# Keys and values of four late heads by seven products of blocks, in a hybrid attention and convolution step

## The chip, the cores and the metric

The kernel runs on one core of one Trainium2 chip. The metric is the device time of one execution in microseconds; the median of the runs shown is compared. In three runs the kernel before took 1614.0 to 1616.18 us, with a median of 1615.59 us.

The engines are called TensorE (PE in the profile, its weight loads PEld), VectorE (DVE), ScalarE (ACT), GpSimd (POOL) and SyncE (SP). SyncE issues the weight loads, GpSimd most other transfers.

## The reference

One step of a decoder layer, for a prompt of 16 learned and 512 given rows and for 8 decoding sequences of 4 rows each, so 560 rows of 2048 columns:

```python
h = rmsnorm(x, g_pre)
q, k, v, ga, cb, cc, ch, gc, ma, mc = jnp.split(h @ w_in, split_offsets(), axis=-1)
a = attend(q, k, v, b_sb).reshape(bsz, t, D_ATTN) * jax.nn.silu(ga)   # 8 heads of 128, stick-breaking
u = cc * ch
c = cb * causal_conv(concat(conv_hist, u), w_conv, b_conv) * jax.nn.silu(gc)
merged = sigmoid(ma + b_gate[:D_MODEL]) * (a @ w_pa) + sigmoid(mc + b_gate[D_MODEL:]) * (c @ w_pc)
y = x + rmsnorm(merged @ w_out, g_post)
return y, k, v, u_ext[:, -(CONV_WIDTH - 1):]
```

`attend` gives key s to query t only for s < t, with the weight sigmoid(z_ts) * prod over s < j < t of (1 - sigmoid(z_tj)). The decoding rows attend to 512 cached keys and values each, in 4 pages of 128, besides their own. The keys and values of all 560 rows are outputs too. Everything is float32.

## The kernel before

**Numbers.** Every float32 operand of a large product is split in two halves that TensorE multiplies fast: `hi` (ScalarE, L240) and `lo = x - hi` (VectorE, L241). Three matmuls (hi hi, hi lo, lo hi) make one product. The split weights have three buffers each (`whl`), the raw weights five (`wraw`); a weight tile is 128 x 1024, eight blocks of 128 rows for 128 output columns.

**Stages.** First the norm fills `h_hi` and `h_lo` (h transposed, 16 blocks of 128 x 560), with the query projections of heads 0 to 3. Then `head_now` for heads 0 to 3: K projection (`k_proj`), V projection (`v_proj`), the query projection of the head that lies four further on, and the attention (`attend`). Then `head_later` for heads 4 to 7: K and V projections alone, K to the scratch `k_scr`, V to `vn_scr`. Such a plain projection (`proj`) computes 128 output columns for 560 rows in two halves of 280: 2 halves x 16 blocks x 3 = 96 matmuls, from two weight tiles.

**Seven products.** Behind the heads come the gates and the convolution's inputs, 72 blocks of 128 columns, in 36 pairs of 256 columns (`pair`, `seven`). A pair is a product of 2 x 2 blocks (rows of h in two halves, inputs in two halves, columns in two halves), and is computed with seven block products instead of eight, each of 8 x 3 = 24 matmuls, 168 a pair. For that three of the right sides are sums of blocks of h, in the tiles `t_hi[i]` and `t_lo[i]`, built once (L906 to L927, on chunks of two of eight blocks, VectorE's sums and ScalarE's `hi`); the fourth, `r1`, is written over block (0, 1) of `h_hi` and `h_lo` at the end. Four weight sums a pair (L953, L956, L964, L969) are made by VectorE, and seven weight tiles are split instead of four.

**The decode's pieces.** The decode attention is a generator (`decode_steps`), called by `dec_step` at many places: in 64 logit steps (each one page of cached keys for one sequence, four rows and four heads: 16 reduces on VectorE, L754), then the weights, then 16 groups of value products and their ends (L841, on TensorE, from `vpage` tiles). `DEC1 = 6` says that the logits of six of the 16 units (a unit has four steps) are made among the heads, and those of the other ten behind each group of gates, by the table in `dec_group`.

**Behind the gates** comes a stage over the 16 column blocks of `w_pc`, with the attention of heads 4 to 7 and the decode's value products between (`head_here`), and then `w_pa`, the merge and `w_out`.

**What sets the order.** The program is written in loops, and a scheduler orders the instructions of each engine when the kernel is built: it moves them past each other where data and buffers allow. On the chip each engine takes its instructions in that order, one behind the other, and waits where an input is not there. So a tile's `hi` and `lo`, the sums and the reduces stand in one queue on VectorE, and a matmul waits for the latest of its operands.

Of the kernel before, what the change touches and what calls it, by code (L numbers as in the profile page):

```python
# [17 lines left out]
P = 128  # L18
# [29 lines left out]
DEC1 = 6  # L48
# [12 lines left out]
def hybrid_step_kernel(  # L61
# [499 lines left out]
    def k_proj(h):  # L561
        o = proj(GATE_K + h * P, ALL)
        kr = hp.tile([P, T], F32, name="raw", bufs=2)
        for ob, s in nparts(o):
            act.copy(kr[:, s], ob)
# [11 lines left out]
    def v_proj(h, pl=None):  # L577
        o = proj(GATE_V + h * P, ALL)
        vr = hp.tile([P, T], F32, name="raw", bufs=2)
        for ob, s in nparts(o):  # L580
            act.copy(vr[:, s], ob)
# [109 lines left out]
    def head_now(h):  # L691
# [7 lines left out]
        q_proj(NOW + h)  # L699
        dec_step(2, "part")  # L700
# [5 lines left out]

    def head_later(h):
        pool.dma_start(k_scr[h], k_proj(h))
        dec_step(2, "part")
        v_proj(h)  # L710
        dec_step(2, "part")
# [20 lines left out]
    def decode_steps():  # L732
# [89 lines left out]
        for g in range(2):  # L822
            for hf in range(2):
                cs = slice(hf * 512, (hf + 1) * 512)
                po = t_ps()
                for pg in range(NPG + 1):
                    if pg < NPG:
                        vts = []
                        for j in range(4):
                            vt = d3.tile([P, 512], F32, name="vpage", bufs=7)  # L830
                            page_load(vt, vc, 4 * g + j, pg, cs)
                            vts.append(vt)
# [37 lines left out]
    def dec_group():  # L870

        n = n_group[0] = n_group[0] + 1
        if n <= 32:
            dec_step((0, 2, 2, 2)[n - 1] if n <= 4 else 1 if n <= 20 else 1 + n % 2, "logits")
# [9 lines left out]
    nctx.close()  # L884
    for h in range(NOW, H):
        head_later(h)
    dec_step(64, "part")
# [5 lines left out]
    for i in range(3):  # L893
        ttp = tctx.enter_context(tc.tile_pool(name=f"tt{i}", bufs=1))
        t_hi.append(ttp.tile([P, 8, HU], F32R, name=f"t_hi{i}"))
        t_lo.append(ttp.tile([P, 8, HU], F32R, name=f"t_lo{i}"))
    h_f, l_f = h_hi.bitcast(F32), h_lo.bitcast(F32)

    def blk(x, i, j):
        return x[:, 8 * i:8 * i + 8, (j + 1) * HC - HU:(j + 1) * HC]  # L900
# [5 lines left out]
    with tc.tile_pool(name="tsum", bufs=2, side="right") as tsp:  # L906
        r1 = tsp.tile([P, 8, HU], F32, name="r1", bufs=1)
        for c in range(0, 8, 2):
# [3 lines left out]
            r, x, y = part(r1), *(tsp.tile([P, 2, HU], F32, name=n) for n in "xy")  # L912
# [14 lines left out]
    hctx.close()  # L927


    def gate_out(j, w, g):  # L930
        pool.dma_start(gate_scr[j][:, w, :], g)

    def gate_bias(j, w):
        return bg[:, KD * w + j:KD * w + j + 1]
# [47 lines left out]
    def pair(c, n):  # L982
# [6 lines left out]
        def rt(i):  # L989
            return lambda k: (t_hi[i][:, k, HU - n:HU], t_lo[i][:, k, HU - n:HU])  # L990
# [3 lines left out]
        yield from seven(ws, n, rb, rt, s, lambda name: sp2.tile([P, HU], F32, name=name)[:, :n])  # L994
# [3 lines left out]
    sp2 = gctx.enter_context(tc.tile_pool(name="sums", bufs=1))  # L998
# [100 lines left out]
    gctx.close()  # L1099
    tctx.close()  # L1100
# [331 lines left out]
```

## Time and profile before

| | us |
|---|---|
| median of three runs | 1615.59 |
| the profiled execution | 1616.69 |
| its span on the chip | 1615.1 |
| TensorE busy | 1595.0 (99%) |
| VectorE busy | 1268.6 (79%) |
| ScalarE busy | 754.0 (47%) |
| mean granted clock of TensorE | 0.997 of full speed |

By time from the span's start: norm and first queries to about 78 us; attention of heads 0 to 3 to about 297; K and V of heads 4 to 7 to about 369; the 36 pairs to about 1112, at some 21 us each for most; the `w_pc` stage with heads 4 to 7 to about 1330; the rest to the end. The busy time of an engine counts overlapping instructions once. The spacing of two neighbouring instructions (start to start) is shorter than a row's duration, since one begins before the other's end is recorded.

### The profile page before, as it was taken

What the parts mean: (1) busy time and instruction counts of PE and PEld (TensorE: products, weight loads), DVE (VectorE), ACT (ScalarE), POOL (GpSimd) and SP (SyncE); (2) the same over time, 40 slices, a digit from 0 to 9 for tenths busy, and PEclk for the clock granted to TensorE, in tenths of its full rate; (3) what the DMA queues carried; (4) which work ended last, traced back from release to release, by engine and by line L of the source; (5) the groups of instructions that cost most, each with busy time, mean ns of one, the idle gap of its engine ahead of it and who ended that gap; (6) DMA issues with size and microseconds to landing.
All of it is one profiled execution on the core that took longest, in us unless ns stands there. A gap on an engine that the chain in (4) does not pass through costs nothing.

```text
span 1615.1 us, 32344 instructions
## 1 busy us (share of the span) xinstructions
PE 1595.0 (99%) x12172; PEld 1533.7 (95%) x12172; DVE 1268.6 (79%) x3574; ACT 754.0 (47%) x1339; POOL 238.0 (15%) x428
## 2 busy tenths in 40 slices
PE   9999999999999999999999999999999999999997
PEld 8999999999999999999999999999757789999997
DVE  6328999947899999999999986667565747887776
ACT  6335554435444444444454444446554523355562
POOL 1133333221111001001011100001322210000000
PEclk9999999999999999999999999999999999999999
DMA  8245555344554445454455544444966755533345
GB/s 244 85 139 179 162 173 177 114 121 142 163 166 138 137 139 164 119 151 133 139 171 183 155 145 128 130 127 124 334 218 222 232 152 162 173 88 110 99 133 187
DMA packets 300675, 252.77 MB, mean 157 GB/s; under 512 B 11522, under 2 KB 268614, under 8 KB 299702
## 3 DMA queue, kind: packets, MB, share of 16 engines
q1 hardware_dynamic: 272021, 160.45, 34.5%
q0 software_dynamic: 28368, 89.98, 16.8%
q8 instruction: 95, 1.56, 0.4%
q14 instruction: 63, 0.51, 0.1%
q10 hardware_dynamic: 128, 0.27, 0.1%
HBM read 217.95 MB, written 32.71 MB: 155 GB/s over the span
## 4 chain that ended last, share of the span: by engine, by line
PE 95%; DMA 2%; DVE 2%; ACT 1%; issue 0%; DVEq 0%; POOL 0%; SPq 0%; ACTq 0%
PE mm L941 31%; PE mm L256 27%; PE o L941 23%; PE tp L841 3%; PE mm L321 2%; PE z L677 1%; PE o L687 1%; PE z L321 1%; PE z L608 1%; PE z L1373 1%; DMA sg<-a_scr 1%; PE tp L505 0%; DMA raw<-in_w_pc 0%; DMA qb<-q_scr 0%; PE z L1227 0%
## 5 line engine op out<-in xcount | busy, mean ns | idle before, releaser
L240 ACT CAST whi<-raw 128x1024 fp32r<-128x1024 f32 x247 | 259.5, 1051 | 385.2 <-PE mm L941 118.5
L241 DVE TENSOR_TENSOR wlo<-raw,whi 128x1024 fp32r<-128x1024 f32 x247 | 301.8, 1223 | 87.8 <-ACT whi L240 86.5
L941 PE MATMUL mm<-h_hi,whi 128*128 128x272 f32 (+1 forms) x1152 | 332.3, 288 | 0.0
L941 PE MATMUL mm<-h_lo,whi 128*128 128x272 f32 (+1 forms) x1152 | 332.3, 288 | 0.0
L941 PE MATMUL mm<-h_hi,wlo 128*128 128x272 f32 (+1 forms) x1152 | 332.3, 290 | 0.0
L941 PE MATMUL o<-t_hi,whi 128*128 128x272 f32 (+1 forms) x864 | 250.1, 289 | 1.6 <-DVE c L967 1.6
L941 PE MATMUL o<-t_lo,whi 128*128 128x272 f32 (+1 forms) x864 | 250.2, 290 | 0.0
L754 DVE CUSTOM_DVE_ANT_0 junk<-kpage,qb 128x128 f32<-128x128 f32 x1024 | 246.3, 288 | 4.7 <-DMA qb<-q_scr 4.3
L941 PE MATMUL o<-t_hi,wlo 128*128 128x272 f32 (+1 forms) x864 | 249.8, 289 | 0.0
L941 PEld LDWEIGHTS mm<-h_hi,whi 128*128 128x128 f32 x1152 | 217.4, 189 | 0.0
L941 PEld LDWEIGHTS mm<-h_hi,wlo 128*128 128x128 f32 x1152 | 216.8, 189 | 0.1
L941 PEld LDWEIGHTS mm<-h_lo,whi 128*128 128x128 f32 x1152 | 216.8, 188 | 0.1
L241 DVE TENSOR_TENSOR wlo<-s,whi 128x1024 fp32r<-128x1024 f32 x126 | 154.4, 1225 | 63.6 <-ACT whi L240 62.4
L240 ACT CAST whi<-s 128x1024 fp32r<-128x1024 f32 x126 | 132.0, 1048 | 153.8 <-PE mm L941 51.7
L256 PE MATMUL mm<-h_lo,whi 128*128 128x280 f32 (+1 forms) x640 | 187.6, 293 | 0.0
L256 PE MATMUL mm<-h_hi,wlo 128*128 128x280 f32 (+1 forms) x640 | 187.1, 293 | 0.0
L256 PE MATMUL mm<-h_hi,whi 128*128 128x280 f32 (+1 forms) x640 | 186.7, 292 | 0.0
L941 PEld LDWEIGHTS o<-t_hi,whi 128*128 128x128 f32 x864 | 163.0, 189 | 2.1 <-DVE c L967 2.0
L941 PEld LDWEIGHTS o<-t_lo,whi 128*128 128x128 f32 x864 | 163.4, 189 | 0.4 <-issue 0.4
L941 PEld LDWEIGHTS o<-t_hi,wlo 128*128 128x128 f32 x864 | 163.1, 189 | 0.1
L256 PEld LDWEIGHTS mm<-h_lo,whi 128*128 128x128 f32 x640 | 120.3, 188 | 0.8
L256 PEld LDWEIGHTS mm<-h_hi,whi 128*128 128x128 f32 x640 | 120.5, 188 | 0.5
(390 smaller groups left out, 3214.5 us busy)
## 6 DMA issues: line engine op xcount, KB each, us to landing
raw<-in_w_in SPq DMA_DIRECT2D x192, 512.0 KB, 4.3
kpage<-in_cache_k POOLq DMA_DIRECT2D x64, 256.0 KB, 3.7
qb<-q_scr POOLq DMA_DIRECT2D x32, 512.0 KB, 5.7
vpage<-in_cache_v POOLq DMA_DIRECT2D x64, 256.0 KB, 5.4
raw<-in_w_out SPq DMA_DIRECT2D x32, 512.0 KB, 4.1
gate_scr<-g POOLq DMA_DIRECT2D x32, 272.0 KB, 4.8
gt<-gate_scr POOLq DMA_DIRECT2D x16, 544.0 KB, 4.5
raw<-in_w_pc SPq DMA_DIRECT2D x16, 512.0 KB, 7.3
```

The source lines that it names most:

```text
L240: act.copy(hi, x)
L241: dve.tensor_sub(lo, x, hi.bitcast(F32))
L256: pe.matmul(o, lhsT=w, rhs=r[:, t0:t1], start=(k == 0 and n == 0), stop=(k == nk - 1 and n == 2))
L321: pin(pe.matmul(o, lhsT=l, rhs=r[:, k, t0:t1], start=(start and m == 0), stop=(stop and m == 2), skip_group_check=True))
L608: pe.matmul(zt[:m, c0:c0 + n], lhsT=l[:, s0:s0 + m], rhs=r[:, ts:ts + n], start=(c0 == 0 and i == 0), stop=(i == 2), skip_group_check=True)
L677: pe.matmul(o, lhsT=l, rhs=x, start=False, stop=(i == len(ops) - 1), skip_group_check=True)
L687: pe.matmul(ot[:, ts - NMETA:ts - NMETA + n], lhsT=l[:m, st, :], rhs=x[:m, c0:c0 + n], start=False, stop=(g == GROUPS[-1] and i == 2), ski ...
L754: dve.tensor_tensor_reduce(out=junk, in0=kt[:, h * P:(h + 1) * P], in1=qt[:, t, h * P:(h + 1) * P], scale=1.0, scalar=0.0, op0=ALU.mult, o ...
L841: pe.matmul(po[32 * j:32 * (j + 1), :], lhsT=lhs, rhs=rhs, start=(pg == 0), stop=(pg == NPG), tile_position=(0, 32 * j), skip_group_check= ...
L941: pe.matmul(o, lhsT=l[:, k, :], rhs=r, start=(start and k == 0 and m == 0), stop=(stop and k == 7 and m == 2), skip_group_check=True)
L1373: pin(pe.matmul(o, lhsT=(m1, m2)[h][:, k + 8 * (q == 1), ts], rhs=two[h][q == 2][:, :, k, :], start=(n == 0), stop=(n == 47)))
```

## The change

- K and V of heads 4 to 7 are no longer computed by `proj` but in four pairs, two heads' K or two heads' V at a time (`two_heads`), by the same `seven` as the gates, on halves of 280 columns. `k_proj` and `v_proj` take their result as an argument.
- For that the t tiles are built on all 560 rows (`HC` = 280 columns for each half instead of `HU` = 274) and the build is written ahead of these pairs; the pool `sums` opens there too.
- The query projections of heads 4 to 7 are written behind the attention of heads 0 to 3, and no longer inside `head_now`.
- `DEC1` falls from 6 to 4: eight logit steps (two units) are no longer made among the heads but with the gates; `dec_group`'s table calls them.
- `vpage` has six buffers instead of seven.

```diff
@@ -45,7 +45,7 @@
 NPG = 4
 NPOOL = 40
 EPS = 1e-6
-DEC1 = 6
+DEC1 = 4
 SCRATCH = 4096
 FIRST = 4
 WARM = 10
@@ -558,11 +558,15 @@
         split_evac(vhi[0:16, 4, :], vlo[0:16, 4, :], vn[0:16, 4, :], vn[0:16, 4, :])
         return vhi, vlo
 
-    def k_proj(h):
-        o = proj(GATE_K + h * P, ALL)
-        kr = hp.tile([P, T], F32, name="raw", bufs=2)
-        for ob, s in nparts(o):
-            act.copy(kr[:, s], ob)
+    def whole(c):
+
+        r = hp.tile([P, T], F32, name="raw", bufs=2)
+        for ob, s in nparts(proj(c, ALL)):
+            act.copy(r[:, s], ob)
+        return r
+
+    def k_proj(h, kr=None):
+        kr = whole(GATE_K + h * P) if kr is None else kr
         kn = hp.tile([P, 5, P], F32, name="nat", bufs=2)
         ks = hp.tile([TS, P], F32, name="ks", bufs=1)
         natural(kr, kn, ks)
@@ -574,11 +578,8 @@
                        bias=bsb[0:TS, h:h + 1])
         return kr
 
-    def v_proj(h, pl=None):
-        o = proj(GATE_V + h * P, ALL)
-        vr = hp.tile([P, T], F32, name="raw", bufs=2)
-        for ob, s in nparts(o):
-            act.copy(vr[:, s], ob)
+    def v_proj(h, pl=None, vr=None):
+        vr = whole(GATE_V + h * P) if vr is None else vr
         vn = hp.tile([P, 5, P], F32, name="nat", bufs=2)
         vs = hp.tile([TS, P], F32, name="ks", bufs=1)
         natural(vr, vn, vs)
@@ -696,19 +697,12 @@
         dec_step(1 if h else 0, "part")
         vhi, vlo = v_proj(h, np_)
         dec_step(1, "part")
-        q_proj(NOW + h)
-        dec_step(2, "part")
+        dec_step(1, "part")
         ot = attend(np_, h, khi, klo, vhi, vlo, qr)
         dec_step(2, "part")
         at = np_.tile([P, PQ], F32, name="at", bufs=1)
         act.copy(at, ot)
         pool.dma_start(a_scr[h], at)
-
-    def head_later(h):
-        pool.dma_start(k_scr[h], k_proj(h))
-        dec_step(2, "part")
-        v_proj(h)
-        dec_step(2, "part")
 
     def head_loads(h):
         kr = hl[0].tile([P, T], F32, name="kr")
@@ -827,7 +821,7 @@
                     if pg < NPG:
                         vts = []
                         for j in range(4):
-                            vt = d3.tile([P, 512], F32, name="vpage", bufs=7)
+                            vt = d3.tile([P, 512], F32, name="vpage", bufs=6)
                             page_load(vt, vc, 4 * g + j, pg, cs)
                             vts.append(vt)
                         if g + hf + pg == 0:
@@ -871,7 +865,7 @@
 
         n = n_group[0] = n_group[0] + 1
         if n <= 32:
-            dec_step((0, 2, 2, 2)[n - 1] if n <= 4 else 1 if n <= 20 else 1 + n % 2, "logits")
+            dec_step((0, 2, 2, 2)[n - 1] if n <= 4 else 1 + n % 2, "logits")
         else:
             dec_step(1)
 
@@ -882,9 +876,9 @@
     for h in range(NOW):
         head_now(h)
     nctx.close()
+    dec_step(64, "part")
     for h in range(NOW, H):
-        head_later(h)
-    dec_step(64, "part")
+        q_proj(h)
 
 
 
@@ -892,24 +886,24 @@
     t_hi, t_lo = [], []
     for i in range(3):
         ttp = tctx.enter_context(tc.tile_pool(name=f"tt{i}", bufs=1))
-        t_hi.append(ttp.tile([P, 8, HU], F32R, name=f"t_hi{i}"))
-        t_lo.append(ttp.tile([P, 8, HU], F32R, name=f"t_lo{i}"))
+        t_hi.append(ttp.tile([P, 8, HC], F32R, name=f"t_hi{i}"))
+        t_lo.append(ttp.tile([P, 8, HC], F32R, name=f"t_lo{i}"))
     h_f, l_f = h_hi.bitcast(F32), h_lo.bitcast(F32)
 
     def blk(x, i, j):
-        return x[:, 8 * i:8 * i + 8, (j + 1) * HC - HU:(j + 1) * HC]
+        return x[:, 8 * i:8 * i + 8, j * HC:(j + 1) * HC]
 
     def t_split(hi, lo, x):
         act.copy(hi, x)
         dve.tensor_sub(lo, x, hi.bitcast(F32))
 
     with tc.tile_pool(name="tsum", bufs=2, side="right") as tsp:
-        r1 = tsp.tile([P, 8, HU], F32, name="r1", bufs=1)
+        r1 = tsp.tile([P, 8, HC], F32, name="r1", bufs=1)
         for c in range(0, 8, 2):
             def part(x, *ij):
                 return (blk(x, *ij) if ij else x)[:, c:c + 2]
 
-            r, x, y = part(r1), *(tsp.tile([P, 2, HU], F32, name=n) for n in "xy")
+            r, x, y = part(r1), *(tsp.tile([P, 2, HC], F32, name=n) for n in "xy")
             dve.tensor_sub(r, part(h_f, 0, 0), part(h_f, 0, 1))
             dve.tensor_add(r, r, part(l_f, 0, 0))
             dve.tensor_sub(r, r, part(l_f, 0, 1))
@@ -924,14 +918,7 @@
             t_split(part(t_hi[2]), part(t_lo[2]), x)
         for c in range(0, 8, 2):
             t_split(blk(h_hi, 0, 1)[:, c:c + 2], blk(h_lo, 0, 1)[:, c:c + 2], r1[:, c:c + 2])
-    hctx.close()
-
-
-    def gate_out(j, w, g):
-        pool.dma_start(gate_scr[j][:, w, :], g)
-
-    def gate_bias(j, w):
-        return bg[:, KD * w + j:KD * w + j + 1]
+
 
     def product(o, w, rhs, start, stop):
         hi, lo = w
@@ -987,15 +974,38 @@
             return lambda k: (h_hi[:, 8 * i + k, slice(*hs[j])], h_lo[:, 8 * i + k, slice(*hs[j])])
 
         def rt(i):
-            return lambda k: (t_hi[i][:, k, HU - n:HU], t_lo[i][:, k, HU - n:HU])
+            return lambda k: (t_hi[i][:, k, HC - n:HC], t_lo[i][:, k, HC - n:HC])
 
         ws = blocks_of(win, c)
         s = sp2.tile([P, 8, P], F32, name="s")
-        yield from seven(ws, n, rb, rt, s, lambda name: sp2.tile([P, HU], F32, name=name)[:, :n])
+        yield from seven(ws, n, rb, rt, s, lambda name: sp2.tile([P, HC], F32, name=name)[:, :n])
+
+    sctx = ExitStack()
+    sp2 = sctx.enter_context(tc.tile_pool(name="sums", bufs=1))
+
+    def two_heads(c):
+
+        rs = [hp.tile([P, T], F32, name="raw", bufs=2) for _ in range(2)]
+        for m, half, ob in pair(c, HC):
+            act.copy(rs[m][:, NMETA + half * HQ:NMETA + (half + 1) * HQ], ob[:, HM:HC])
+            act.copy(rs[m][:, half * HM:(half + 1) * HM], ob[:, 0:HM])
+        return rs
+
+    for h in range(NOW, H, 2):
+        for i, r in enumerate(two_heads(GATE_K + h * P)):
+            pool.dma_start(k_scr[h + i], k_proj(h + i, r))
+        for i, r in enumerate(two_heads(GATE_V + h * P)):
+            v_proj(h + i, vr=r)
+    hctx.close()
+
+    def gate_out(j, w, g):
+        pool.dma_start(gate_scr[j][:, w, :], g)
+
+    def gate_bias(j, w):
+        return bg[:, KD * w + j:KD * w + j + 1]
 
     gctx = ExitStack()
     gp = gctx.enter_context(tc.tile_pool(name="gates", bufs=2))
-    sp2 = gctx.enter_context(tc.tile_pool(name="sums", bufs=1))
 
 
     UP, US = PQ + 2, DB * (DT + 2)
@@ -1097,6 +1107,7 @@
     dec_step(64, "values")
     assert "values" in dec_at and "end" not in dec_at
     gctx.close()
+    sctx.close()
     tctx.close()
```

The whole program has 96 matmuls of TensorE less, 36 instructions of VectorE more (12 splits, 16 weight sums, 8 differences `c`) and 24 of ScalarE more; the number of transfers on SyncE's and GpSimd's queues is the same.

The order on VectorE, before, while K and V of heads 4 to 7 are projected. L913 to L923 are the t sums, L904 the `lo` of a t tile, L241 the `lo` of a weight tile:

```order
L915 TENSOR_TENSOR r_5282<-r_5282,h_lo 128x548 x3
L241 TENSOR_TENSOR wlo<-raw,whi 128x1024
L915 TENSOR_TENSOR r_5282<-r_5282,h_lo 128x548
L916 TENSOR_TENSOR x<-r_5282,h_hi 128x548 x2
L241 TENSOR_TENSOR wlo<-raw,whi 128x1024
L917 TENSOR_TENSOR x<-x,h_lo 128x548 x2
L919 TENSOR_TENSOR y<-h_hi,x 128x548 x2
L904 TENSOR_TENSOR t_lo_5268<-x,t_hi_5267 128x548
L920 TENSOR_TENSOR y<-y,h_lo 128x548
```

With the change, the end of the same build, between the last splits of the first K pair and the first split of the second (L907 to L917 are the sums, L898 the `lo` of a t tile, L940 and L951 weight sums):

```order
L241 TENSOR_TENSOR wlo<-s,whi 128x1024
L898 TENSOR_TENSOR t_lo_3850<-x,t_hi_3849 128x560 x2
L940 TENSOR_TENSOR s<-raw 128x1024
L910 TENSOR_TENSOR x<-r_3854,h_hi 128x560 x2
L951 TENSOR_TENSOR raw<-raw 128x1024
L911 TENSOR_TENSOR x<-x,h_lo 128x560 x2
L241 TENSOR_TENSOR wlo<-raw,whi 128x1024
L913 TENSOR_TENSOR y<-h_hi,x 128x560 x2
L898 TENSOR_TENSOR t_lo_3840<-x,t_hi_3839 128x560 x2
L914 TENSOR_TENSOR y<-y,h_lo 128x560 x2
L916 TENSOR_TENSOR x<-h_hi,x 128x560 x2
L898 TENSOR_TENSOR t_lo_3845<-y,t_hi_3844 128x560
```

The t sums stood between the splits of plain projections, whose matmuls read no t tile; now they stand between the splits of a pair whose matmuls read them.

On TensorE, with the change, from the last products of head 3's attention (L688) into the first K pair (L928; L256 is the last query projection):

```order
L688 MATMUL o<-hiA,vhi 128x512
L256 MATMUL mm<-h_hi,wlo 128x272
...
L688 MATMUL o<-loA,vhi 128x512
L688 MATMUL o<-hiA,vlo 128x512
L256 MATMUL mm<-h_hi,whi 128x272
...
L928 MATMUL mm<-h_hi,whi 128x280
L928 MATMUL mm<-h_lo,whi 128x280
L928 MATMUL o<-t_hi_3839,whi 128x280
L928 MATMUL mm<-h_hi,wlo 128x280
```

Before, the rows behind `o<-loA` were matmuls of K and V projections (L256, `mm<-h_hi,whi 128x280`); now a dozen of the last query projection and then the pair, whose third product is the first to read a t tile.

On TensorE in the `w_pc` stage, with the change (L835 is L841 of before, a value product; L256 is `w_pc`):

```order
L256 MATMUL mm<-c_hl,whi 128x272
L835 MATMUL tp<-vpage,z_all 32x512
L256 MATMUL mm<-c_hl,whi 128x272
L256 MATMUL mm<-c_hl,wlo 128x272
L256 MATMUL mm<-c_hl,whi 128x272 x2
L256 MATMUL mm<-c_hl,wlo 128x272
L835 MATMUL tp<-vpage,z_all 32x512
L835 MATMUL tp<-v_new,z_new 32x512 x4
```

The 80 value products stand in 40 groups of neighbours before and in 44 with the change.

## The prediction

> **What bounds the kernel now.** I read the page first (busy time by engine, then the chain that ended last), then TensorE's waits, then windows stage by stage, and at last single stretches of VectorE's timeline.
>
> ```profile
> span 1615.1 us, 32344 instructions
> PE 1595.0 (99%) x12172; PEld 1533.7 (95%) x12172; DVE 1268.6 (79%) x3574; ACT 754.0 (47%) x1339; POOL 238.0 (15%) x428
> PE 95%; DMA 2%; DVE 2%; ACT 1%; issue 0%; DVEq 0%; POOL 0%; SPq 0%; ACTq 0%
> ```
>
> TensorE is busy 99% of the span and makes 95% of the chain, so time falls only where its own work falls, and rises wherever something makes it wait. VectorE's 79% is an average over stages. TensorE's waits on VectorE between 150 and 1330 us come to two rows:
>
> ```profile
> PE mm L256 <- DVE gt L1148: 3.3, 1, 3.3
> PE o L941 <- DVE c L967: 1.6, 2, 0.8
> ```
>
> (total us, times, longest.) Next the windows. Columns: span, then busy us and count of PE, weight load, VectorE, ScalarE and GpSimd, then granted clock, DMA share, GB/s.
>
> ```profile
> 167.00:308.00 141.00, 141.00 (x1079) 137.10 (x1077) 136.49 (x720) 71.89 (x143) 48.68 (x87) 1.00 0.53 160
> 294.30:336.70 42.40, 42.40 (x332) 41.75 (x331) 39.20 (x61) 18.45 (x38) 11.47 (x19) 1.00 0.43 127
> 350.00:363.60 13.60, 13.60 (x108) 13.35 (x107) 2.93 (x4) 3.88 (x10) 3.39 (x6) 1.00 0.39 117
> 430.00:950.00 520.00, 518.40 (x4103) 517.74 (x4102) 499.87 (x1687) 232.11 (x343) 54.63 (x95) 1.00 0.50 149
> 950.00:1100.00 150.00, 150.00 (x1194) 150.00 (x1194) 101.28 (x97) 72.89 (x105) 7.59 (x14) 1.00 0.44 133
> 1150.00:1200.00 50.00, 46.74 (x251) 29.74 (x245) 28.73 (x63) 20.81 (x36) 13.82 (x26) 0.97 0.81 257
> ```
>
> The first row is the attention of the early heads: VectorE is at 136.5 of 141 us, so it follows TensorE closely without yet holding it. The third is a plain projection of a late head: VectorE works 2.9 of 13.6 us there. The fourth is most of the seven-product pairs with the logits among them, VectorE at 499.9 of 520 and TensorE hardly waiting. The second is the stretch in which the twelve sums of h (the t tiles) are built now: VectorE is at 39.2 of 42.4 us, all of it under TensorE's late K and V projections.
>
> **The change part by part. What it removes.** The instruction order counts 768 matmuls of 280 columns less (eight plain projections of 96) and 672 more (four pairs of seven products of 24): 96 fewer. The 350 to 363.6 row gives 13.60/108 = 0.126 us each, so 96 x 0.126 = **-12.1 us** of TensorE. With nothing waiting this would be the whole effect.
>
> **What it moves: the t sums.** The pairs of K and V need the t tiles, which until now nothing needed before the first gate pair. The order (section on the change) shows where they now stand: behind the last splits of head 3's attention and between the weight splits of the first K pair, all on VectorE, which takes its instructions in order. TensorE in the same place goes from head 3's output product straight through the last query projection into that pair. VectorE's prices come from its timeline now:
>
> ```profile
> 290.86 0.69 DVE L495 TENSOR_TENSOR loA<-eA,hiA 128x512 fp32r<-128x512 f32 x1
> 293.37 0.29 DVE L754 CUSTOM_DVE_ANT_0 junk<-kpage,qb 128x128 f32<-128x128 f32 x1
> 293.58 0.29 DVE L754 CUSTOM_DVE_ANT_0 junk<-kpage,qb 128x128 f32<-128x128 f32 x1
> 294.34 2.65 DVE L913 TENSOR_TENSOR r<-h_hi 128x548 f32<-128x548 f32 x4
> 296.91 1.36 DVE L914 TENSOR_TENSOR r<-r,h_lo 128x548 f32<-128x548 f32 x2
> 301.78 1.20 DVE L241 TENSOR_TENSOR wlo<-raw,whi 128x1024 fp32r<-128x1024 f32 x1
> 302.91 0.71 DVE L915 TENSOR_TENSOR r<-r,h_lo 128x548 f32<-128x548 f32 x1
> 309.19 0.73 DVE L904 TENSOR_TENSOR t_lo<-x,t_hi 128x548 fp32r<-128x548 f32 x1 [0.59 <-ACT t_hi L903]
> 335.90 0.73 DVE L904 TENSOR_TENSOR t_lo<-x,t_hi 128x548 fp32r<-128x548 f32 x1 [0.86 <-ACT t_hi L903]
> ```
>
> Start to start, four sums take 296.91 - 294.34 = 2.57 us, 0.643 each at 548 columns, 0.657 at the new 560. A split or add of 128x1024 takes 302.91 - 301.78 = 1.13 us. From behind `loA` of head 3 up to and with the first weight split of the second K pair, the new order holds 43 of the sums and 11 operations of 128x1024 (7 splits, 4 weight sums): 43 x 0.657 + 11 x 1.13 = 28.2 + 12.4 = 40.7 us of VectorE. TensorE between the product that reads `loA` and the matmul that reads that split has 161 instructions, 161 x 0.126 = 20.3 us. So TensorE comes 20.4 us early, less the lead that VectorE has when it starts. In the kernel before that lead can be read off: `loA` is done at 290.86 + 0.69 = 291.55, and its reader starts here:
>
> ```profile
> 294.97 0.39 PE L687 MATMUL o<-loA,vhi 128*128 128x512 f32 x1
> ```
>
> That is 3.4 us. After the change seven t sums stand ahead of `loA` (7 x 0.657 = 4.6 us), so I expect less of it, between 0 and 3.4; I take 1.7, the middle. On the other side VectorE itself waits for ScalarE's halves of the splits: two such waits, 0.59 and 0.86 us, are quoted above, and up to 2 us of them may stand in the pair. That makes 17.0 to 22.4; I take **+19 us**. What is late next: the second product of the next pair, the chunks of the t tiles, then the splits behind them. All these gaps lie in the one VectorE queue, so they add to the 19 and not to more. After it VectorE catches up: a pair is 168 x 0.126 = 21.2 us of TensorE and 11 x 1.13 = 12.4 us of splits and sums. The cover that made the same build free before was eight projections of about 12 us with only two splits each, as the 350 to 363.6 row shows; it is exactly the work that the change turns into pairs.
>
> [...]
>
> **The clock.** The 3.3 us wait in the list stands at 1154, and its window (1150 to 1200) has a granted clock of 0.97, where the others have 1.00: 0.03 x 50 = 1.5 us of slow matmuls behind one long idle. The new stall is several gaps, one or two of them longer than that. Bounds 0 and 3 us; I take **+1**.
>
> **Heads 0 to 3.** The query projections of heads 4 to 7 leave the attention (4 x 96 x 0.126 = 48 us of TensorE, with 8 splits, 9 us of VectorE), and eight logit steps of 16 reduces leave it too: the junk rows start 293.58 - 293.37 = 0.21 us apart, so 8 x 16 x 0.21 = 27 us. VectorE loses 36 us, TensorE 48, where they stood at 136.5 to 141: the ratio goes slightly up, and VectorE's lead before a split goes down. Bounds 0 and +4 us; I take 0, since the 167 to 308 row shows no wait at such a load.
>
> **The logits at the gates.** The 128 reduces do not come on top of full pairs. The order's count of reduces per pair is the same up to the 26th gate pair (16 to 32); the 27 us go to the five pairs behind, at 31 or 32 per pair. Those lie in the 950 to 1100 row, VectorE 101.3 of 150 us: 14.2 per pair and 31 x 0.21 = 6.5 more make 20.7 of 21.2. The pairs just ahead already run so in the 430 to 950 row without a wait. Taken 0; if the cover fails, at most the two-us kind of the second wait row.
>
> **The value products.** `vpage` has 6 buffers instead of 7 behind the gates, so the decode's value products stand in smaller groups. In the chain of waits between 1130 and 1345 us:
>
> ```profile
> 1187.28 1.97 PE tp L841 x10
> 1194.15 0.98 PE tp L841 x2
> 1247.80 0.99 PE tp L841 x8
> ```
>
> One alone (two records) costs 0.98 us, four together 0.99, five 1.97. The order has 40 groups of them before and 44 after; counted in steps of four, 46 and 48. Bounds 0 and +4; I take 48 - 46 = **+2 us**.
>
> **At nothing**: 24 more ScalarE copies (ScalarE at 47%; if they were exposed, some 0.5 us each) and the query projections' own loads, stores and transposes, which keep their number and lie under TensorE's matmuls; the number of DMAs on both queues is unchanged.
>
> **The sum**, on the profiled execution (1616.69 us, 1.1 above the median of 1615.59): 1616.69 - 12.1 + 19 + 1 + 2 = 1626.6; on the scale of the median **1625.5 us**. All low ends (17, 0, 0, 0) and all high ends (22.4, 3, 4, 4) give 1620.5 and 1637 on that scale; they won't all fall together, so the forecast's own range is 1620 to 1632.
>
> **The rivals.** (a) *The build stays hidden, faster.* If VectorE entered the first K pair far enough ahead, or the stall were given back, only -12.1 + 2 would be left: 1605.5. It decides once VectorE's lead reaches 20 us. For it: the same 42 us of build cost TensorE nothing before, and VectorE waited there for work:
>
> ```profile
> 341.02 1.23 DVE L241 TENSOR_TENSOR wlo<-raw,whi 128x1024 fp32r<-128x1024 f32 x1 [2.29 <-ACT whi L240]
> 364.21 0.28 DVE L510 COPY nat<-tp 16x128 f32<-16x128 f32 x1 [5.90 <-PE tp L509]
> ```
>
> Against it: three buffers of split weights hold a lead to a few us, and the sums themselves stand in the pair's queue. 0.14.
> (b) *Half of it is hidden, no change.* If the query projections of heads 4 to 7 run late enough for VectorE to begin the sums some 8 us earlier than I read, the stall is 10 to 12 us and the time 1616 to 1618. 0.11.
> (c) *The heads starve as well, slower still.* Without the query projections between them, each of four attentions waits 3 us for VectorE's softplus sums: +12, 1637. It decides where VectorE's 136.5 of 141 becomes more than 141. 0.08.
> [...]
> That the change does not do what it says is no case: the order counts the 96 matmuls.
>
> **How the numbers follow.** Forecast 0.64, (a) 0.14, (b) 0.11, (c) 0.08, (d) 0.03. A difference of 0.2%, some 3.2 us, is about what a measurement of this kernel can tell from none. Faster is (a), 0.14; within it is (b), 0.11; slower the rest, 0.75. The range 1612 to 1633 takes in the forecast's own, (b) and (d), and leaves out (a) and most of (c), about 0.2.
>
> **What would show it.** In the changed profile: TensorE's busy time some 12 us less; waits for `wlo` and the t tiles of 17 to 22 us between head 3's last output product and the second K pair, VectorE without a gap there; a granted clock under 1 just behind; no waits in the gate pairs; a value-product stage 2 us longer. I am wrong if TensorE goes through the first K pair without gaps, or if new waits stand in the heads or the gates.

## The result and the profile after

The changed kernel takes 1623.5 us in the median of five runs (1621.81 to 1625.51), against 1615.59 us before: 7.9 us more by the medians, and 0.55% by the ratio (1.0055, 95% interval 1.0042 to 1.0068). The forecast was 1625.5. The profiled execution took 1624.66 us, 1.2 above the median, with a span of 1623.1. Three executions of those below (one with two plain K projections, one of the half change, one of the kernel before) took over 2000 us; they count in the medians, but not in the ratios.

The page of the changed kernel, busy times and the chain by engine:

```profile
PE 1589.6 (98%) x12076; PEld 1523.3 (94%) x12076; DVE 1302.2 (80%) x3610; ACT 770.1 (47%) x1363; POOL 247.1 (15%) x428
PE 87%; DVE 5%; DMA 3%; issue 2%; ACT 1%; POOL 1%; POOLq 1%; DVEq 0%; SPq 0%; ACTq 0%
```

TensorE has the 96 matmuls less and is busy 5.4 us less (not 12, since slow matmuls count as busy), yet the span is 8.0 longer; its share of the chain falls from 95% to 87%, and VectorE's rises from 2% to 5%. Nearly all new waiting of TensorE is in one place. Its waits between 75 and 375 us (total, times, longest), with the new line numbers (L928 is a product of `seven`, L241 and L240 the halves of a split weight, L898 and L897 those of a t tile, L678 head 0's triangular product):

```profile
PE mm L928 <- DVE wlo L241: 4.8, 2, 2.9
PE mm L928 <- ACT whi L240: 2.9, 2, 2.0
PE o L928 <- DVE t_lo L898: 2.5, 1, 2.5
PE o L928 <- ACT t_hi L897: 1.9, 1, 1.9
PE z L678 <- ACT l L494: 0.8, 1, 0.8
```

The first four add up to 12.1 us, and all lie in the first K pair; the fifth is new too, in head 0. The windows of the changed kernel, for the heads, that pair, the other three pairs, the gates and the `w_pc` stage (columns as in the prediction):

```profile
75.70:262.00 186.30, 185.43 (x1407) 179.10 (x1406) 150.34 (x687) 101.10 (x207) 71.40 (x115) 1.00 0.48 142
262.00:303.20 41.20, 29.20 (x183) 27.59 (x182) 39.94 (x56) 18.19 (x32) 1.62 (x3) 0.83 0.22 65
303.20:373.40 70.20, 70.20 (x550) 69.10 (x549) 45.71 (x52) 33.83 (x66) 16.60 (x28) 1.00 0.48 140
373.40:1144.40 771.00, 769.13 (x6089) 767.19 (x6088) 699.25 (x2155) 361.49 (x527) 89.26 (x154) 1.00 0.52 155
1144.40:1333.20 188.80, 186.17 (x1139) 134.69 (x1138) 108.58 (x240) 88.56 (x151) 45.33 (x82) 0.99 0.70 223
```

and the stages of the gates and of `w_pc` in the kernel before (its 36 pairs end at 1140 us, not at about 1112 as said above):

```profile
369.30:1140.20 770.90, 769.30 (x6082) 767.62 (x6081) 676.42 (x1899) 361.30 (x527) 78.45 (x136) 1.00 0.50 148
1140.20:1325.80 185.60, 182.34 (x1138) 133.99 (x1137) 108.23 (x240) 87.75 (x151) 44.99 (x82) 0.99 0.72 227
```

In the first K pair TensorE is busy 29.2 of 41.2 us, VectorE 39.9. The gates take 771.0 us against 770.9, with 23 us more of VectorE's work in them, and the `w_pc` stage 188.8 against 185.6.

The stages before the gates (from the first plain projection to the first gate pair) grow from 291.0 to 297.7 us, the gates by 0.1, the `w_pc` stage by 3.2 and the rest by 0.6: 10.6 us in all. Norm and first queries, which the change does not touch, ended at 78.3 us in the one execution and at 75.7 in the other; in the runs below this start varies between 74.6 and 78.3 with any kernel. So only stages are compared across executions here, and for whole kernels the medians.

### The profile page after: what moved, and what is told of

Its sections match the earlier page's. It is cut to its first block, busy times and chain, and to the rows that moved or that the text cites. A ratio compares the mean times of both kernels' runs of the same rounds, so it can differ in the third digit from the quotient of the medians.

```text
span 1623.1 us, 32226 instructions
## 1 busy us (share of the span) xinstructions
PE 1589.6 (98%) x12076; PEld 1523.3 (94%) x12076; DVE 1302.2 (80%) x3610; ACT 770.1 (47%) x1363; POOL 247.1 (15%) x428
## 4 chain that ended last, share of the span: by engine, by line
PE 87%; DVE 5%; DMA 3%; issue 2%; ACT 1%; POOL 1%; POOLq 1%; DVEq 0%; SPq 0%; ACTq 0%
PE mm L928 33%; PE o L928 25%; PE mm L256 17%; PE tp L835 3%; PE mm L321 1%; PE z L678 1%; PE z L321 1%; PE o L688 1%; DMA qb<-q_scr 1%; DVE wlo L241 1%; DMA raw<-in_w_in 1%; PE z L609 1%; PE z L1384 1%; DVE junk L748 1%; POOLq L723 1%
## 5 line engine op out<-in xcount | busy, mean ns | idle before, releaser
L240 ACT CAST whi<-raw 128x1024 fp32r<-128x1024 f32 x247 | 259.3, 1051 | 378.2 <-PE mm L928 134.1
L928 PE MATMUL mm<-h_hi,wlo 128*128 128x272 f32 (+2 forms) x1280 | 371.0, 291 | 4.8 <-DVE wlo L241 4.8
L928 PE MATMUL mm<-h_hi,whi 128*128 128x272 f32 (+2 forms) x1280 | 371.1, 290 | 2.9 <-ACT whi L240 2.9
L928 PE MATMUL mm<-h_lo,whi 128*128 128x272 f32 (+2 forms) x1280 | 370.5, 289 | 0.0
L241 DVE TENSOR_TENSOR wlo<-raw,whi 128x1024 fp32r<-128x1024 f32 x247 | 301.5, 1221 | 81.8 <-ACT whi L240 77.3
L928 PE MATMUL o<-t_hi,whi 128*128 128x272 f32 (+2 forms) x960 | 279.3, 291 | 3.7 <-DVE c L954 1.9
L928 PE MATMUL o<-t_lo,whi 128*128 128x272 f32 (+2 forms) x960 | 278.8, 290 | 2.5 <-DVE t_lo L898 2.5
L928 PE MATMUL o<-t_hi,wlo 128*128 128x272 f32 (+2 forms) x960 | 279.1, 291 | 0.0
L928 PEld LDWEIGHTS mm<-h_hi,wlo 128*128 128x128 f32 x1280 | 241.5, 189 | 5.4 <-DVE wlo L241 5.2
L928 PEld LDWEIGHTS mm<-h_hi,whi 128*128 128x128 f32 x1280 | 242.5, 189 | 3.5 <-ACT whi L240 3.5
L928 PEld LDWEIGHTS mm<-h_lo,whi 128*128 128x128 f32 x1280 | 241.6, 189 | 0.1
L240 ACT CAST whi<-s 128x1024 fp32r<-128x1024 f32 x138 | 144.8, 1049 | 162.4 <-PE mm L928 55.7
L241 DVE TENSOR_TENSOR wlo<-s,whi 128x1024 fp32r<-128x1024 f32 x138 | 168.9, 1224 | 63.1 <-ACT whi L240 61.2
L928 PEld LDWEIGHTS o<-t_hi,whi 128*128 128x128 f32 x960 | 182.0, 190 | 4.7 <-DVE c L954 2.5
L928 PEld LDWEIGHTS o<-t_lo,whi 128*128 128x128 f32 x960 | 181.9, 190 | 3.2 <-DVE t_lo L898 2.8
L928 PEld LDWEIGHTS o<-t_hi,wlo 128*128 128x128 f32 x960 | 181.7, 189 | 0.2
L256 PE MATMUL mm<-h_hi,whi 128*128 128x280 f32 (+1 forms) x384 | 112.3, 293 | 0.0
L256 PE MATMUL mm<-h_hi,wlo 128*128 128x280 f32 (+1 forms) x384 | 112.2, 293 | 0.0
L256 PE MATMUL mm<-h_lo,whi 128*128 128x280 f32 (+1 forms) x384 | 112.1, 292 | 0.0
L256 PE MATMUL mm<-c_hl,whi 128*128 128x272 f32 x512 | 105.8, 296 | 2.3 <-DVE gt L1159 2.3
L256 PEld LDWEIGHTS mm<-c_hl,whi 128*128 128x128 f32 x512 | 83.1, 190 | 24.7 <-issue 21.0
```

Source lines behind the costliest of these rows:

```text
L240: act.copy(hi, x)
L241: dve.tensor_sub(lo, x, hi.bitcast(F32))
L256: pe.matmul(o, lhsT=w, rhs=r[:, t0:t1], start=(k == 0 and n == 0), stop=(k == nk - 1 and n == 2))
L928: pe.matmul(o, lhsT=l[:, k, :], rhs=r, start=(start and k == 0 and m == 0), stop=(stop and k == 7 and m == 2), skip_group_check=True)
```

## Did VectorE's queue set the stall? The step taken from both sides

The main step of the forecast can be read almost as it was written. VectorE's and then TensorE's rows of the changed kernel, at the two ends of the stretch that was counted (`loA` of head 3 to the first split of the second K pair):

```profile
257.24 0.68 DVE L495 TENSOR_TENSOR loA<-eA,hiA 128x512 fp32r<-128x512 f32 x1
257.84 0.73 DVE L908 TENSOR_TENSOR r<-r,h_lo 128x560 f32<-128x560 f32 x1
268.02 0.73 DVE L911 TENSOR_TENSOR x<-x,h_lo 128x560 f32<-128x560 f32 x1
268.68 0.73 DVE L913 TENSOR_TENSOR y<-h_hi,x 128x560 f32<-128x560 f32 x1
297.32 1.22 DVE L241 TENSOR_TENSOR wlo<-raw,whi 128x1024 fp32r<-128x1024 f32 x1
298.46 1.39 DVE L898 TENSOR_TENSOR t_lo<-x,t_hi 128x560 fp32r<-128x560 f32 x2
261.72 0.40 PE L688 MATMUL o<-loA,vhi 128*128 128x512 f32 x1
300.41 0.28 PE L928 MATMUL mm<-h_hi,wlo 128*128 128x280 f32 x1
```

VectorE needs 298.46 - 257.84 = 40.6 us for the stretch (40.7 forecast), a sum every 0.66 us. TensorE needs 300.41 - 261.72 = 38.7 us for what is 20.3 us of work: a stall of 18.4. The lead was 261.72 - 257.92 = 3.8 us, so VectorE alone accounts for 40.6 - 20.3 - 3.8 = 16.5 of it.

The other 1.9 us are TensorE's: VectorE is through with the split at 298.5, and TensorE, behind with matmuls at half speed, reads it at 300.4.

Two things could still make this a coincidence: the clock was down in the same place, and weight tiles came late from ScalarE. Two windows of two microseconds in the pair:

```profile
282.00:284.00 2.00, 1.69 (x7) 1.69 (x8) 2.00 (x4) 0.00 (x0) 0.00 (x0) 0.50 0.00 0
290.00:292.00 2.00, 0.41 (x2) 0.41 (x3) 2.00 (x4) 0.00 (x0) 0.00 (x0) 0.50 0.47 127
```

The pair's granted clock is 0.83 on the mean, and matmuls run at half speed for some 14 us of it (0.17 of 41.2 us, twice; the expectation below says 17). So sums were taken out, and logits put in.

**Fewer sums.**

```diff
-            dve.tensor_add(r, r, part(l_f, 0, 0))
-            dve.tensor_sub(r, r, part(l_f, 0, 1))
...
-            dve.tensor_add(x, x, part(l_f, 1, 1))
...
-            dve.tensor_add(y, y, part(l_f, 0, 0))
...
-            dve.tensor_add(x, x, part(l_f, 1, 0))
```

> Left out: the five sums with h_lo in the build of the t tiles (20 of its 52 operations on VectorE), so the t tiles lack the low halves. Theory (VectorE's one queue: TensorE waits in the first K pair because 43 sums stand in it): 17 of the 43 fall away, 17 x 0.657 = 11.2 us, the wait of 18 us in that pair falls to 4 to 7, the time to 1610 to 1613. Rival (the wait comes from what else the trace shows there, the granted clock at 0.5 for 17 us and late weight tiles through ScalarE): the sums hardly matter, 1621 to 1624.

Measured: 1612.17 us, 11.3 less than the change. The kernel before, run beside this and the later runs, had medians of 1614.53, 1614.38 and 1614.09 us, not 1615.59, so a difference from the change's 1623.5 is good to about 1 us. The profiled execution of this run was its slowest, 7.2 us above the median; only its first K pair is read here, from the last product of head 3:

```profile
267.00:297.20 30.20, 25.94 (x188) 24.25 (x187) 27.46 (x37) 17.51 (x31) 1.63 (x3) 1.00 0.30 88
```

11.0 us less than 41.2, for 11.2 us of sums taken away, and the clock is at 1.00 with nothing else changed: the slow clock was a consequence of the waits. Late weight tiles were not the cause either, since the run leaves ScalarE's weight splits as they are and the stall falls by what the sums took; of the 4.3 us of idling that remain, though, 3.1 are waits for ScalarE's `whi`. The slow clock also did not come on top. The changed kernel's pair holds 12.0 us of idling and 183 matmuls that took 29.2 us instead of 23.1, 6.1 us of slow matmuls; if those had counted in full, this run would have gained 17. TensorE ran slowly while it was waiting for VectorE in any case.

**More in the queue.**

```diff
-DEC1 = 4
+DEC1 = 6
...
-            dec_step((0, 2, 2, 2)[n - 1] if n <= 4 else 1 + n % 2, "logits")
+            dec_step((0, 2, 2, 2)[n - 1] if n <= 4 else 1 if n <= 20 else 1 + n % 2, "logits")
```

> The eight logit steps are among the heads again (DEC1 6 and the old table), all else as in the change. Theory: 128 reduces x 0.213 = 27 us more stand in VectorE's queue ahead of the build, and TensorE's wait in the first K pair grows by about as much: 1646 to 1654. Rival (VectorE has 150 of 186 us busy in heads 0 to 3, so 36 us of room takes the steps in): 1622 to 1627.

Measured: 1653.86 us, 30.4 more than the change. TensorE's longest wait in that run:

```profile
298.93 0.60 PE L928 MATMUL mm<-h_hi,whi 128*128 128x280 f32 x1 [23.45 <-ACT h_hi L897]
```

It is the split of `r1` over block (0, 1) of h, behind the reduces and the sums. The 36 us in which VectorE is not busy in heads 0 to 3 take none of it in: 31 of them lie in head 0, whose row stands below, far ahead of the sums' place. Moving the eight logit steps is what keeps the change at 0.5%.

## Could the cover be put elsewhere?

The next two runs keep VectorE's work and change TensorE's.

```diff
+                    if held[0] and k == n == 0:
+                        tc.add_manual_dep(ins.ins, held[0], mybir.DependencyInfo(
+                            mybir.DependencyClass.NoSync, mybir.DependencyReason.DATA), reason="held")
...
+    behind = next(i for i in reversed(nc.cur_bb.bb.instructions) if i.engine == pe.engine)
     for h in range(NOW, H):
+        held[0] = behind.name if h >= 6 else None
         q_proj(h)
```

> The query projections of heads 6 and 7 are held behind the last product of head 3's attention (their first matmuls get an order behind it), so that some 180 matmuls lie under the build. Theory (VectorE's work from head 3's attention to the second K pair is simply more than TensorE's): the cover is taken from head 3, whose softplus chain then holds TensorE for some 15 us, the wait in the K pair falls to about 3; sum 17 to 20 us, time 1622 to 1627. Rival (only the place of the cover is wrong): 22 us of cover put the wait to nothing, 1605 to 1609.

Measured: 1627.64 us, 0.6 above what the theory gave. Head 3's attention, and the first K pair, in that run:

```profile
225.00:258.00 33.00, 22.23 (x122) 18.43 (x121) 31.95 (x128) 13.98 (x28) 10.03 (x14) 0.71 0.24 73
283.10:309.40 26.30, 23.86 (x172) 23.39 (x171) 22.36 (x27) 11.82 (x23) 1.65 (x3) 0.94 0.33 94
```

The pair is down to 26.3 us, but in head 3 TensorE is now busy 22 of 33 us at a clock of 0.71, with VectorE at 32 of 33. The wait has moved to where the cover was taken, and 4 us were lost on the way. In both places together VectorE simply has more to do than TensorE.

```diff
+    for h in (NOW, NOW + 1):
+        pool.dma_start(k_scr[h], k_proj(h))
...
-        for i, r in enumerate(two_heads(GATE_K + h * P)):
+        for i, r in enumerate(two_heads(GATE_K + h * P) if h > NOW else ()):
```

> K of heads 4 and 5 as two plain projections (192 matmuls, four splits) instead of the first pair (168, seven splits, four weight sums), ahead of the build. Theory: the build lies under 192 matmuls x 0.126 = 24 us that read no t tile, with 11 - 4 = 7 operations of 1.13 us fewer on VectorE; the wait goes to 0 to 1 us at the price of 24 x 0.126 = 3.0 us: 1623.5 - 18 + 3 = 1608.5 (1606 to 1611), faster than the kernel before. Rival (clock and weight loads): 1623.5 + 3 = 1626.

Measured: 1615.5 us, 8.0 less than the change, where 15 were expected: no difference from the kernel before (ratio 0.9998, 0.9988 to 1.0008). The rival (1626) falls, but the theory lacks 7 us. The windows of this run, head 0 and then the first pair that reads t tiles (now V of heads 4 and 5); head 0 of the change and of the kernel before; and the one long wait of this run in head 0:

```profile
78.10:149.00 70.90, 68.02 (x490) 64.93 (x490) 37.23 (x145) 32.90 (x75) 26.50 (x42) 0.95 0.51 150
297.00:324.00 27.00, 25.12 (x181) 24.43 (x180) 21.47 (x25) 12.66 (x25) 2.37 (x4) 0.94 0.34 100
```

```profile
75.70:141.50 65.80, 64.93 (x491) 62.31 (x490) 34.52 (x122) 32.93 (x75) 26.44 (x42) 1.00 0.54 157
```

```profile
78.30:156.70 78.40, 78.40 (x606) 76.28 (x605) 44.03 (x188) 36.30 (x80) 24.28 (x47) 1.00 0.53 158
```

```profile
PE z L678 <- ACT raw L565: 2.3, 1, 2.3
```

In the kernel before, TensorE goes through head 0 without a wait. In the change its 491 matmuls there are busy for 64.93 us at a clock of 1.00, and it idles 0.9. This run takes 70.9 us for 490, 6.0 more than that busy time: 2.9 of idling, 2.3 of it one wait for head 0's softplus, and behind that wait the clock falls, 0.95 over the whole 70.9 us, some 3.5 more. The V pair has 1.9 us of idling and a clock of 0.94. Its longest gap is not VectorE's queue but ScalarE's, where a copy that waits for TensorE's own product stands ahead of the split that TensorE needs next:

```profile
304.31 0.39 ACT L948 COPY s<-mm 128x280 f32<-128x280 f32 x1 [2.93 <-PE mm L930]
304.60 1.05 ACT L240 CAST whi<-s 128x1024 fp32r<-128x1024 f32 x1
305.75 0.37 PE L930 MATMUL o<-t_hi,whi 128*128 128x280 f32 x1 [1.47 <-issue]
```

The profiled execution was 4.0 us above this kernel's median, so the two places do not add up exactly to the 7 us; between 78 and 370 us the trace shows no third place of that size.

## The parts alone, on the kernel before

**Query projections.** In `head_now` the line `q_proj(NOW + h)` goes, and a loop over heads 4 to 7 calls it ahead of `head_later`.

> The kernel before with one part of the change alone: the query projections of heads 4 to 7 are written behind the attention of heads 0 to 3, ahead of the plain K and V projections. Same instructions on every engine but one row of order. Theory as forecast (heads 0 to 3 lose cover they don't need): 1613 to 1616, no change. Rival (head 0's softplus chain loses its cover, as the trace of the run with two plain K projections shows: a 2.3 us wait and 6.7 us at half clock there): 1617 to 1622.

Measured: 1617.07 us against 1614.38 of the kernel before on the same chip (ratio 1.0014, 1.0005 to 1.0023): 2.7 us more by the medians and 2.3 by the ratio, at the low end of the rival's range. Head 0 of that run, TensorE's wait there, and the rows of VectorE and ScalarE that lead up to it:

```profile
75.70:144.90 69.20, 67.45 (x491) 64.99 (x490) 36.98 (x143) 32.93 (x75) 26.43 (x42) 0.95 0.52 153
129.82 0.29 DVE L753 CUSTOM_DVE_ANT_0 junk<-kpage,qb 128x128 f32<-128x128 f32 x1 [3.48 <-DMA qb<-q_scr]
130.25 0.30 DVE L651 TENSOR_TENSOR r<-r 128x144 f32<-128x144 f32 x1
130.59 0.54 ACT L494 CAST l<-r 128x416 fp32r<-128x416 f32 x1 [4.17 <-DVE r L651]
131.18 0.46 PE L677 MATMUL z<-l,neg_one 128*128 128x272 f32 x2 [1.75 <-ACT l L494]
```

69.2 us are 4.3 over the 64.9 of busy time above, in an execution that was 3.3 above the median. So the move does cost something, at head 0 alone (the other three heads show no gap). The rows tell why. VectorE is idle there, but its queue is held: a logit reduce waits 3.48 us for a transfer of the decode's queries (`qb`), and the softplus sum `r` stands behind it; ScalarE and TensorE wait in turn. All six traces in which the query projections are moved have such a wait of 2.5 to 3.8 us in head 0; the traces of the kernel before, of the half change and of the next two runs have none above 0.3. That the move brings the reduces forward against the transfer is read from the rows; no run tries it by itself. How much it costs differs between executions: TensorE's waits of 0.5 and 0.85 us there (in the held run and in the change) left the clock at 1.00, waits of 1.6 to 2.3 us brought half clock behind them.

**Logits.** DEC1 4 and the new table alone.

> The kernel before with the eight logit steps moved to the gates alone (DEC1 4 and the new table). Theory: 27 us of VectorE leave heads 0 to 3, where nothing waits for them, and lie in five gate pairs with room: 1613 to 1616. Rival (full pairs hold TensorE there, 0.8 us a wait as in the row of c L967): 1617 to 1620.

Measured: 1614.17 against 1614.38 us (ratio 1.0001, 0.9989 to 1.0013). No change, as forecast.

**vpage.** `bufs=7` becomes `bufs=6`.

> The kernel before with vpage in six buffers instead of seven, nothing else. Theory: the value products fall from 40 groups into 44 (46 to 48 steps of four) at 0.98 us each: +2 to +3.5 us, 1617 to 1619. Rival (the longer stage over w_pc in the changed kernel comes from something else, as the time at which the gates' last transfers end): 1614 to 1616.

Measured: 1617.04 against 1614.38 us (ratio 1.0011, 1.0001 to 1.0021), 1.8 by the ratio and 2.7 by the medians. The stage, then the value products in the stage in this run, in the change and in the kernel before (busy us, mean ns):

```profile
1140.30:1329.30 189.00, 185.99 (x1139) 134.56 (x1138) 108.48 (x240) 88.62 (x151) 44.78 (x82) 0.99 0.70 222
L841 PE MATMUL tp<-vpage,z_all 128*32 128x512 f32 x128 | 44.9, 604 | 0.0
```

```profile
L835 PE MATMUL tp<-vpage,z_all 128*32 128x512 f32 x128 | 44.9, 604 | 0.0
```

```profile
L841 PE MATMUL tp<-vpage,z_all 128*32 128x512 f32 x128 | 42.4, 603 | 0.0
```

With six buffers alone the stage takes 189.0 us, as in the change (188.8), and 2.5 us more of it are value products. The forecast's +2 is this.

## Two versions that are faster

If the stall is VectorE's surplus over a stretch, more plain projections under the build remove it, at 24 matmuls a pair. And if a lone value product costs as much as four, their order is worth far more than the change.

```diff
+        if h in (0, 1, 2, 3):
+            q_proj(NOW + h)
...
-                            vt = d3.tile([P, 512], F32, name="vpage", bufs=6)
+                            vt = d3.tile([P, 512], F32, name="vpage", bufs=7)
...
-        q_proj(h)
+        if h - NOW not in (0, 1, 2, 3):
+            q_proj(h)
+    for h in (NOW, NOW + 1):
+        pool.dma_start(k_scr[h], k_proj(h))
+        v_proj(h)
...
-    for h in range(NOW, H, 2):
+    for h in range(NOW + 2, H, 2):
...
-        us_ = [gp.tile([P, UP + US], F32, name="u", bufs=2) for _ in range(2)]
+        us_ = [up_.tile([P, UP + US], F32, name="u", bufs=2) for _ in range(2)]
...
-    for i in range(0, 8, 2):
-        conv_pair(i)
+    with tc.tile_pool(name="conv", bufs=1) as up_:
+        for i in range(0, 8, 2):
+            conv_pair(i)
```

> Half of the change: only K and V of heads 6 and 7 in pairs; K and V of heads 4 and 5 plain and ahead of the build, the query projections of heads 4 to 7 within heads 0 to 3 as before, the logits moved as in the change, vpage in seven buffers (room by a pool of its own for the convolution's u). 48 matmuls fewer than the kernel before, 6.0 us. Theory: the build lies under 384 matmuls that read no t tile, no wait in the pairs, heads 0 to 3 as before: 1614.5 to 1615.6 - 6.0 = 1608 to 1611. Rival (in the pairs of K and V something else than the build costs time): 1612 to 1616.

Measured: 1609.52 us, ratio 0.9968 (0.9954 to 0.9981): faster than before by 5.2 us by the ratio, 6.0 forecast. Its plain K and V behind head 3, and its two pairs:

```profile
287.30:313.10 25.80, 25.80 (x202) 25.46 (x201) 24.24 (x36) 14.58 (x30) 6.49 (x11) 1.00 0.31 96
313.10:360.40 47.30, 46.12 (x360) 45.36 (x359) 34.48 (x40) 23.08 (x44) 8.32 (x14) 1.00 0.43 126
```

VectorE is at 24.2 of 25.8 us, nearly as full as in the change, and TensorE has no gap there, because what it does meanwhile reads no t tile. The two pairs behind idle 1.2 us, for ScalarE's `whi`.

The order of the value products, on the kernel before and then on this half change:

```diff
-                    for j in range(4):
+                    for j in (3, 0, 1, 2):
...
-                        pe.matmul(po[32 * j:32 * (j + 1), :], ...)
+                        ins = pe.matmul(po[32 * j:32 * (j + 1), :], ...)
+                        if j < 3:
+                            pin(ins)
```

> The kernel before, with the four value products of a page group in another order: the product of the page that is loaded last comes first, the other three are pinned behind it, so that the order holds them in 20 groups (23 steps of four) instead of 40 (46). Same instructions and transfers. Theory (a step costs TensorE 0.98 us whether one product stands in it or four, the term of +2 us in the forecast): 23 x 0.98 = 22.5 us less, 1592 to 1597 with up to 4 us of waits for the last page. Rival (the steps are where TensorE would wait in any case, for the head's softplus or for w_pc): 1612 to 1616.

> The half change (K and V of heads 6 and 7 in pairs) with the same order of the value products and vpage in eight buffers: 19 groups, 22 steps. Theory: 24 x 0.98 = 23.5 us off the 1609.5 of the half change, 1585 to 1591, the fastest so far. Rival as for the other: 1607 to 1610.

Measured: 1600.46 us on the kernel before (ratio 0.9906, 0.9889 to 0.9923), a gain of 13.6 us by the medians against 1614.09 and 15.2 by the ratio, less than the 1592 to 1597 expected; and 1585.11 us on the half change (ratio 0.9817, 0.98 to 0.9833), as expected. The `w_pc` stage with its value products, of the first and of the second:

```profile
1138.90:1309.50 170.60, 161.59 (x1139) 133.17 (x1138) 108.04 (x240) 88.38 (x151) 45.26 (x82) 0.97 0.76 246
L841 PE MATMUL tp<-vpage,z_all 128*32 128x512 f32 x128 | 19.1, 605 | 1.4 <-DMA vpage<-in_cache_v 1.3
```

```profile
1131.40:1293.60 162.20, 156.10 (x1138) 130.34 (x1137) 108.32 (x240) 87.12 (x151) 44.67 (x81) 0.99 0.81 259
L837 PE MATMUL tp<-vpage,z_all 128*32 128x512 f32 x128 | 17.9, 604 | 1.1 <-issue 1.1
```

The products' busy time falls from 42.4 to 19.1 and 17.9 us. With seven buffers the stage gains 15.0 us of the 22.5 expected: TensorE idles 9.0 us in it instead of 3.3 at a clock of 0.97, so part comes back as waits. On the half change, with eight buffers, it takes 162.2 us instead of 186.0, 23.8 less, all that was expected; no run has the new order there with seven buffers, so what the eighth adds is not separated. Four value products that stand next to each other take 0.99 us in the kernel before, one alone 0.98 (the rows quoted in the prediction), so the gain needs an order that places them next to each other: the same 128 products of `vpage` are busy for 42.4 us with the value products in 40 groups of the order and for 19.1 with 20.

## Why the prediction was right, point by point

- **96 matmuls, -12.1.** TensorE has exactly these fewer. They show in the stages ahead of the gates: 6.7 us longer with 12.1 less of work, so 18.8 us of new waiting and slow matmuls.
- **The t sums, +19 (17.0 to 22.4).** The stall is in the place named, by the queue named, and VectorE's count held (40.6 for 40.7). The whole stall is 18.4 us, but that holds the clock's 1.9; VectorE alone gave 16.5, just under the bounds. The lead was 3.8 us, outside the 0 to 3.4 that I allowed (the sums ahead of `loA` did not eat it up), and the waits of VectorE for ScalarE, for which up to 2 us were allowed, did not come.
- **The clock, +1 (0 to 3).** 1.9 us at the end of the stretch, and no more, though 6.1 us of matmul time were lost to the clock. As a term of its own its size was half of what it came to; that most of a slow clock vanishes under a wait for another engine was not in the forecast. With the t sums it makes 18.4 where 20 were forecast.
- **Heads 0 to 3, taken 0 (0 to +4).** A zero that did not hold: in the change TensorE idles 0.9 us in head 0, and the move alone cost 2.3 us by the ratio. The row of 167 to 308 us on which I rested it holds no head 0. In that head VectorE is busy for only 34.5 of 65.8 us; what is late is its queue, held by a reduce that waits for a transfer. A new wait in the heads was one of the signs of being wrong that the forecast named; it came, and is small.
- **Logits at the gates, taken 0.** 771.0 against 770.9 us with them, and no change alone.
- **Value products, +2 (0 to +4).** 2.5 us of products, 3.2 in the stage.
- **Rivals.** (a) needed a lead of 20 us; it was 3.8. The two rows quoted for it, VectorE waiting at 341 and 364 us, lie behind the stretch of the build (294.3 to 336.7), in which VectorE is busy for 39.2 of 42.4 us, and so told nothing of its room there. (b) asked that later query projections would cover the sums; held later by hand, they only move the wait. (c) named four heads and too much work for VectorE; it was one head and a transfer in VectorE's queue, at a fifth of the price. (d), at 0.03, was that VectorE's operations do not overlap. The sums follow each other every 0.66 us and last 0.73. At the durations in the rows (0.73 for a sum, 1.22 for a split) the stretch would have taken 43 x 0.73 + 11 x 1.22 = 44.8 us, an estimate; the trace has 40.6.

The sum was 1626.6 for the profiled execution, which took 1624.66. By stages the change costs 10.6 us, against 9.9 forecast, so no large error hides another; but its execution also started 2.6 us earlier (75.7 against 78.3 us), and whether that is chance cannot be told from two executions.

## What to carry to other kernels

An algorithm with fewer products trades TensorE's time for sums on another engine, and what it is worth is settled where those sums stand: count them in that engine's queue between two instructions that TensorE needs, against TensorE's own work between the same two, and take off only the lead that the trace shows. If the queue is longer (here 40.6 us against 20.3 and a lead of 3.8), moving cover along it moves the wait (1627.64 us with two query projections held); work that reads none of the sums (no gap in 25.8 us on the half change), or fewer sums (11.0 us less for 11.2 taken away), removes it. Before adding waits and slow clock as two terms, ask which engine sets the end of the stretch, and look at each repetition of a stage, the first above all, before resting a zero on one window. An engine that is idle for half of a stage can still be the late one there, when an instruction in its queue waits for a transfer (VectorE in head 0 with the query projections alone: busy for 37.0 of 69.2 us, and held for 3.48).

## What the runs showed of the hardware that I had not expected

A wait of TensorE well below the 3.3 us one that I had priced the clock by can be followed by half clock: 2.3 us (0.95 over head 0 with two plain K projections) and 1.75 us, while waits of 0.5 and 0.85 us in the same place left it at 1.00. The windows around the 1.75 us one, in the run with the query projections alone:

```profile
128.00:131.00 3.00, 1.44 (x12) 1.21 (x10) 1.18 (x10) 0.41 (x1) 0.00 (x0) 1.00 0.83 271
131.00:134.00 3.00, 2.82 (x13) 2.43 (x13) 3.00 (x18) 1.95 (x5) 1.02 (x2) 0.62 0.10 31
134.00:137.00 3.00, 3.00 (x13) 2.94 (x13) 3.00 (x20) 1.33 (x3) 2.99 (x3) 0.50 0.27 96
137.00:140.00 3.00, 3.00 (x19) 2.81 (x19) 2.10 (x18) 1.76 (x5) 2.62 (x6) 0.74 0.60 175
```

Over these nine microseconds behind the wait the clock lacks 0.38, 0.50 and 0.26 of three each, 3.4 us. The length of a wait alone does not decide, though. In the first K pair of the change a wait of 1.87 us left the clock at 1.00; half clock began only behind 3.4 us in which TensorE was busy for 0.52:

```profile
272.38 0.40 PE L928 MATMUL mm<-h_hi,wlo 128*128 128x280 f32 x1 [1.87 <-DVE wlo L241]
271.50:275.00 3.50, 2.62 (x20) 2.62 (x21) 3.50 (x5) 0.98 (x3) 0.00 (x0) 1.00 0.02 5
278.40:281.80 3.40, 0.52 (x2) 0.30 (x2) 3.40 (x6) 2.10 (x5) 0.00 (x0) 1.00 0.67 178
281.80:285.20 3.40, 2.89 (x12) 2.89 (x13) 3.40 (x5) 0.02 (x1) 0.00 (x0) 0.50 0.00 0
```

Half clock lasts 3.4 us there, some 10 in the second stretch of the same pair (288.6 to 298.8), and 6.8 behind the 1.75 us wait (3.4 us lost are 6.8 at half clock). So a small wait cost 3.4 us more here (behind 1.75 us) or none (behind 0.5, 0.85 and 1.87 us), which may be why the executions of such a kernel spread; neither that nor what decides was tried by itself.

Four value products in a row cost 0.99 us and a single one 0.98 in the kernel before. Ordering them so was worth some 15 us on the kernel before, and 24 on the half change together with an eighth buffer, three times what the change cost.
